# Hybrid decoder trunk on one core: the first norm's gain spread by GpSimd into SBUF instead of by one-row products into PSUM

## The chip, the core and the metric

The kernel runs on one core of a Trainium2 chip. The metric is the device time of one execution in microseconds (us), as the median of several runs; the inputs lie in the chip's memory at the start and the output has to be there at the end.

## What is computed

Two layers work on 256 rows of 1024 float32 values. Each layer is a half-weighted gated feed-forward block, a mixing block (retention, block attention and convolution heads side by side), and a second feed-forward block; a norm stands ahead of each block and one at the end. Cut to what the change touches:

```python
def rms_norm(x, g):
    y = x * lax.rsqrt(jnp.mean(x * x, -1, keepdims=True) + EPS)
    return y * g

for l in range(DEPTH):                                   # DEPTH = 2
    h = rms_norm(x, ffn1_norm[l])
    x = x + 0.5 * (jax.nn.silu(h @ ffn1_wg[l]) * (h @ ffn1_wu[l])) @ ffn1_wd[l]
    h = rms_norm(x, mix_norm[l])
    x = x + mix(h @ w_in[l], ...) @ w_out[l]
    h = rms_norm(x, ffn2_norm[l])
    x = x + 0.5 * (jax.nn.silu(h @ ffn2_wg[l]) * (h @ ffn2_wu[l])) @ ffn2_wd[l]
return rms_norm(x, final_norm)
```

The change lies in the very first `rms_norm`: its `g` is a vector of 1024 values that multiplies every row, so each of the 128 partitions needs a copy of it.

## The kernel before

The 256 rows are two tiles `x0` and `x1` of 128 partitions by 1024. Weights are float32 and come as "raw" buffers (three of them, up to 1 MB each) on SyncE's queue; ScalarE makes a rounded high part of each (`whi`), VectorE the remainder (`wlo`), and TensorE multiplies with both. All engines follow a written order in the opening; TensorE does so throughout.

The opening is `setup` and `start`. `setup` sets a small constant on GpSimd (`mhalf`), starts the loads of `x0` and `x1` in halves on SyncE's queue, and loads the gain (`row`, one partition of 1024) and the identity (`ident`) on ScalarE's queue. `start` then

- issues dummy products on TensorE (`spin`, a bf16 tile of ones `z` times itself), between them two one-row products, `ones` times `row`, that put the gain on 128 partitions in two PSUM banks `g[0]`, `g[1]` (line 260), and one more dummy;
- takes the sums of squares of each half tile on ScalarE (`stats`, line 271), and from them the row factor `r` on GpSimd in three small instructions, `e`, `e` and `r` (lines 272 to 274);
- multiplies x by `r` and `g` on VectorE (`rows`, line 280, output `xr`, one half tile each; there is one buffer `xr`, so the second tile's first half must wait until the transposes have read the first tile);
- transposes `xr` on TensorE (`turn`, line 286), and makes the high and low parts of the transposed rows, `hT` (lines 294 and 298);
- starts the first weight products (`prod`, line 326), with the eight pieces of the first two raw buffers split by lines 314 and 318.

After the opening the feed-forward block goes on with `single` and `down`, fed by `pump` (lines 147 and 148).

Of the kernel before, what the change touches and what calls it, by code (L numbers as in the profile page):

```python
# [11 lines left out]
F32 = mybir.dt.float32  # L12
# [8 lines left out]
D = 1024  # L21
S = 256
P = 128
# [32 lines left out]
class Kernel:  # L56
# [144 lines left out]
    def mm3(self, out, ah, al, wh, wl, start, stop):  # L201
        mm = self.nc.tensor.matmul
        mm(out, ah, wh, start=start, stop=False)  # L203
        mm(out, ah, wl, start=False, stop=False)  # L204
        mm(out, al, wh, start=False, stop=stop)  # L205

    def mm2w(self, out, wh, wl, x, start, stop):
        mm = self.nc.tensor.matmul
        mm(out, wh, x, start=start, stop=False)  # L209
        mm(out[:, :S], wl, x[:, 0], start=False, stop=stop)  # L210
# [12 lines left out]
    def setup(self):  # L223
        nc, c, a = self.nc, self.const, self.a
        self.mhalf = c.tile([P, 8], F32, tag="mhalf", name="mhalf")
        nc.gpsimd.memset(self.mhalf, -0.5)
        warm = c.tile([P, 8], F32, tag="warm", name="warm")
        nc.scalar.activation(warm, self.mhalf, AF.Silu)
        self.x = [c.tile([P, D], F32, tag=f"x{t}", name=f"x{t}") for t in range(NT)]
        for t in range(NT):  # L230
            for h in range(2):
                n = slice(h * 512, (h + 1) * 512)
                nc.sync.dma_start(self.x[t][:, n], a["x"][t][:, n])
        self.row = self.act.tile([P, D + 8], F32, tag="g", bufs=1, name="row")[0:1, :D]
        nc.scalar.dma_start(self.row, a["fgain"][0:1])
        self.ident = self.load("ident", (P, P), eng=nc.scalar)

# [1 line left out]
    def start(self, st):  # L241
        nc, mm = self.nc, self.nc.tensor.matmul
# [2 lines left out]
        n[0]["xr"] = n[0]["tile"]()  # L245
        sqs = [self.act.tile([P, 512], BF16, tag="sq", bufs=1, name=self.name("sq"))]
        z = self.scratch(BF16)
        ones = self.scratch()
        nc.vector.memset(z, 1.0)
        nc.vector.memset(ones[0:1, :P], 1.0)  # L250
        idle = self.mmb()

        def spin(n):
            for _ in range(n):
                mm(idle, z[:, :P], z, start=True, stop=True)

        spin(4)
        g = [self.acc() for _ in range(2)]
        for h in range(2):
            mm(g[h], ones[0:1, :P], self.row[:, h * 512:(h + 1) * 512], start=True, stop=True)  # L260
        spin(1)
        while len(self.raws) < RBUFS:
            self.fetch()

# [871 lines left out]
```

## Time and profile before

| | |
|---|---|
| median of 3 runs | 991.15 us (990.84 to 991.24) |
| profiled execution, its own time | 988.81 us |
| its span, first to last instruction | 987.0 us |
| TensorE busy | 976.8 us, 99% of the span |
| VectorE busy | 683.8 us, 69% |
| ScalarE busy | 537.1 us, 54% |
| GpSimd busy | 67.5 us, 7% |

The profiled execution took 1.8 us more than its span. A busy share near 100% on TensorE means that nearly every microsecond holds some product; it doesn't say that the product was needed, since the dummies of the opening count as well.

### The profile page before, as it was taken

How to read it: one execution, taken by the hardware profiler on the slowest of the kernel's cores; microseconds unless marked ns; L12 is line 12 of the kernel's file. 1: busy time of each engine (PE TensorE's matmuls, PEld its weight loads, DVE VectorE, ACT ScalarE, POOL GpSimd, SP SyncE). 2: the span in 40 equal slices, each digit the busy share in tenths (PEclk: the TensorE clock that was granted, in tenths of full speed). 3: DMA queues.
4: the chain of work that ended last, by engine and by line, in shares of the span. 5: the costliest groups of instructions: out<-in, count | busy, mean ns of one | idle time of the engine just before them, and what ended most of it. 6: DMA issues, size and time to landing. Idle time of an engine off the chain costs nothing.

```text
span 987.0 us, 13779 instructions
## 1 busy us (share of the span) xinstructions
PE 976.8 (99%) x5321; PEld 850.1 (86%) x5321; DVE 683.8 (69%) x1030; ACT 537.1 (54%) x904; POOL 67.5 (7%) x115
## 2 busy tenths in 40 slices
PE   9999999999999999999999999999999999999997
PEld 6888888898998888888888888888989888888885
DVE  5987565669976866666676656566799677666653
ACT  5755555366554755555465555554665456555542
POOL 0101000021140000000000000002100400000000
PEclk9999999999999999999999999999999999999999
DMA  7975555345542855555546464543545346555511
GB/s 258 334 273 178 205 180 180 119 152 190 171 171 70 309 199 174 208 175 206 176 183 223 171 210 173 205 142 136 193 144 199 135 151 254 176 208 173 209 45 43
DMA packets 28580, 180.17 MB, mean 183 GB/s; under 512 B 3425, under 2 KB 3809, under 8 KB 10338
## 3 DMA queue, kind: packets, MB, share of 16 engines
q1 hardware_dynamic: 27216, 175.54, 51.1%
q10 hardware_dynamic: 1298, 3.74, 1.0%
q8 instruction: 42, 0.69, 0.3%
q14 instruction: 24, 0.20, 0.1%
HBM read 178.22 MB, written 1.05 MB: 182 GB/s over the span
## 4 chain that ended last, share of the span: by engine, by line
PE 92%; DVE 5%; ACT 1%; DMA 1%; issue 1%; POOL 0%; SPq 0%; POOLq 0%; ACTq 0%; DVEq 0%
PE mm L209 15%; PE tr L209 15%; PE acc L614 8%; PE acc L613 8%; PE acc L617 8%; PE tr L210 8%; PE mm L210 8%; PE mm L203 4%; PE mm L205 4%; PE mm L204 4%; DVE wlo L148 2%; DVE ac L866 2%; PE acc L209 1%; PE mm L326 1%; PE tr L505 1%; PE acc L809 1%
## 5 line engine op out<-in xcount | busy, mean ns | idle before, releaser
L148 DVE TENSOR_TENSOR wlo<-raw,whi 128x1024 fp32r<-128x1024 f32 (+1 forms) x340 | 397.9, 1181 | 172.8 <-ACT whi L147 168.9
L147 ACT ACTIVATE whi<-raw 128x1024 fp32r<-128x1024 f32 (+1 forms) x340 | 344.0, 1023 | 213.1 <-PE acc L617 84.7
L209 PE MATMUL mm<-hT,whi 128*128 128x512 f32 x640 | 226.1, 391 | 0.0
L209 PE MATMUL tr<-hT,whi 128*128 128x512 f32 x640 | 225.9, 391 | 0.0
L210 PE MATMUL tr<-hT,wlo 128*128 128x256 f32 x640 | 180.5, 282 | 0.0
L210 PE MATMUL mm<-hT,wlo 128*128 128x256 f32 x640 | 180.4, 282 | 0.0
L209 PEld LDWEIGHTS mm<-hT,whi 128*128 128x128 f32 x640 | 120.1, 188 | 25.9
L209 PEld LDWEIGHTS tr<-hT,whi 128*128 128x128 f32 x640 | 120.1, 188 | 25.1
L613 PE MATMUL acc<-whi,hf 128*128 128x512 f32 x352 | 137.7, 391 | 0.0
L614 PE MATMUL acc<-wlo,hf 128*128 128x512 f32 x352 | 137.2, 390 | 0.0
L210 PEld LDWEIGHTS mm<-hT,wlo 128*128 128x128 f32 x640 | 120.8, 189 | 1.4
L210 PEld LDWEIGHTS tr<-hT,wlo 128*128 128x128 f32 x640 | 121.0, 189 | 0.0
L617 PE MATMUL acc<-whi,hf 128*128 128x512 f32 x352 | 113.6, 389 | 0.0
L203 PE MATMUL mm<-whi,hT 128*128 128x384 f32 (+1 forms) x272 | 99.3, 365 | 0.0
L205 PE MATMUL mm<-whi,hT 128*128 128x384 f32 (+1 forms) x272 | 94.2, 346 | 0.0
L204 PE MATMUL mm<-wlo,hT 128*128 128x384 f32 (+1 forms) x272 | 94.1, 346 | 0.0
L617 PEld LDWEIGHTS acc<-whi,hf 128*128 128x128 f32 x352 | 66.1, 188 | 13.9
L599 ACT ACTIVATE s<-part 128x256 f32<-128x256 f32 x80 | 33.2, 416 | 82.2 <-DVE part L215 82.0
L613 PEld LDWEIGHTS acc<-whi,hf 128*128 128x128 f32 x352 | 66.1, 188 | 13.6
L614 PEld LDWEIGHTS acc<-wlo,hf 128*128 128x128 f32 x352 | 66.2, 188 | 12.3
L215 DVE TENSOR_TENSOR part<-part,tr 128x256 f32<-128x256 f32 x80 | 33.5, 419 | 47.3 <-ACT part L214 47.3
L866 DVE SCALAR_TENSOR_TENSOR ac<-u,vec,ac 128x256 f32<-128x256 f32 x120 | 56.6, 525 | 0.0
(179 smaller groups left out, 983.2 us busy)
## 6 DMA issues: line engine op xcount, KB each, us to landing
raw<-in_wgb SPq DMA_DIRECT2D x80, 1024.0 KB, 4.9
raw<-in_wd SPq DMA_DIRECT2D x44, 1024.0 KB, 4.9
raw<-in_win SPq DMA_DIRECT2D x28, 768.0 KB, 5.1
raw<-in_wout SPq DMA_DIRECT2D x8, 1024.0 KB, 4.9
raw<-in_wga SPq DMA_DIRECT2D x6, 1024.0 KB, 5.4
raw<-in_wcv SPq DMA_DIRECT2D x4, 1024.0 KB, 5.0
raw<-in_wga SPq DMA_DIRECT2D x8, 256.0 KB, 5.6
g<-in_fgain ACTq DMA_DIRECT2D x3, 512.0 KB, 3.9
```

The source lines that it names most:

```text
L147: nc.scalar.activation(hi[:, c], src, AF.Copy)
L148: nc.vector.tensor_tensor(lo[:, c], src, hi[:, c].bitcast(F32), op=OP.subtract)
L203: mm(out, ah, wh, start=start, stop=False)
L204: mm(out, ah, wl, start=False, stop=False)
L205: mm(out, al, wh, start=False, stop=stop)
L209: mm(out, wh, x, start=start, stop=False)
L210: mm(out[:, :S], wl, x[:, 0], start=False, stop=stop)
L215: self.nc.vector.tensor_tensor(v, lo, ps[:, :S], op=OP.add)
L613: mm(ys[t][h], hi[:, ts], wh[:, n], start=first, stop=False)
L614: mm(ys[t][h], hi[:, ts], wl[:, n], start=False, stop=False)
L617: mm(ys[t][h], lo[:, ts], wh[:, n], start=False, stop=last)
L866: nc.vector.scalar_tensor_tensor(ac[ct], us, wj, ac[ct], op0=OP.mult, op1=OP.add)
```

## The change

The gain is now loaded as two rows of 512 into two scratch buffers, each by its own transfer on ScalarE's queue, and GpSimd's `partition_broadcast` copies each row to 128 partitions of an SBUF tile `g0`. The two one-row products, their PSUM banks and the tile `ones` are gone. `ident` is loaded behind the two rows. TensorE has 14 dummies in one piece, where it had four, the one-row products and one.

```diff
-        self.row = self.act.tile([P, D + 8], F32, tag="g", bufs=1, name="row")[0:1, :D]
-        nc.scalar.dma_start(self.row, a["fgain"][0:1])
-        self.ident = self.load("ident", (P, P), eng=nc.scalar)
+        self.g0 = self.act.tile([P, D + 8], F32, tag="g", bufs=1, name="g0")[:, :D]
...
         z = self.scratch(BF16)
-        ones = self.scratch()
         nc.vector.memset(z, 1.0)
-        nc.vector.memset(ones[0:1, :P], 1.0)
+        g = []
+        for h in range(2):
+            row = self.scratch()[0:1]
+            nc.scalar.dma_start(row, self.a["fgain"][0:1, h * 512:(h + 1) * 512])
+            g.append(self.g0[:, h * 512:(h + 1) * 512])
+            nc.gpsimd.partition_broadcast(g[h], row)
+        self.ident = self.load("ident", (P, P), eng=nc.scalar)
         idle = self.mmb()
...
-        spin(4)
-        g = [self.acc() for _ in range(2)]
-        for h in range(2):
-            mm(g[h], ones[0:1, :P], self.row[:, h * 512:(h + 1) * 512], start=True, stop=True)
-        spin(1)
+        spin(14)
```

GpSimd's row before, from `mhalf` to the row factors of both tiles. An `ISA` row without a tile here is the instruction that selects the library of GpSimd code; it is not written in the kernel but put in by the compiler.

```order
L226 MEMSET mhalf 128x8
L272 ISA
L272 TENSOR_SCALAR e_127<-ss_126 128x1 [waits Activation_49]
L273 TENSOR_TENSOR e_127<-ss_126,e_127 128x1 [waits Activation_49,Pool_49]
L274 TENSOR_TENSOR r_128<-e_127,mhalf 128x1 [waits Pool_49]
L272 TENSOR_SCALAR e_136<-ss_135 128x1 [waits Activation_49]
```

The same place after the change; the two `ISA` rows with `g` are the broadcasts, each of which waits for its row's transfer.

```order
L226 MEMSET mhalf 128x8
L252 ISA
L252 ISA g_84<-hf_90 128x512 [waits DMAHW3_49]
L252 ISA g_84<-hf_93 128x512 [waits DMAHW5_49]
L271 ISA
L271 TENSOR_SCALAR e_135<-ss_134 128x1 [waits Activation_49]
L272 TENSOR_TENSOR e_135<-ss_134,e_135 128x1 [waits Activation_49,Pool_49]
L273 TENSOR_TENSOR r_136<-e_135,mhalf 128x1 [waits Pool_49]
L271 TENSOR_SCALAR e_144<-ss_143 128x1 [waits Activation_49]
```

Ahead of the first `e` there now stand two broadcasts and a second selection: library 1 for the broadcasts, library 0 again for what follows, as before.

SyncE's queue before, the first loads of x and of the weights (`raw`); what a row waits for is the landing of an earlier transfer that used the same counter.

```order
L233 DMA x_78<-in_x 128x512 x2
L233 DMA x_79<-in_x 128x512 x2
L129 DMA raw_105<-in_wga 128x512 x2
L129 DMA raw_105<-in_wga 128x512 [waits DMAHW0_49]
L129 DMA raw_105<-in_wga 128x512 [waits DMAHW1_49]
L129 DMA raw_110<-in_wga 128x512 [waits DMAHW2_49]
```

The same place after the change.

```order
L233 DMA x_78<-in_x 128x512 x2
L233 DMA x_79<-in_x 128x512 x2
L129 DMA raw_113<-in_wga 128x512
L129 DMA raw_113<-in_wga 128x512 [waits DMAHW0_49]
L129 DMA raw_113<-in_wga 128x512 [waits DMAHW1_49]
L129 DMA raw_113<-in_wga 128x512 [waits DMAHW2_49]
```

ScalarE issues three transfers where it issued two, so the counters come round one place earlier: the second to fourth weight piece now each wait for the half of x one place later (counters 0 to 3 belong to the halves of x and to the gain's row). Behind the opening the engines' orders are the same in both kernels.

## Rows read from the trace of the kernel before

**Rows 1.** The page: span, busy time by engine, the chain that ended last.
```profile
span 987.0 us, 13779 instructions
PE 976.8 (99%) x5321; PEld 850.1 (86%) x5321; DVE 683.8 (69%) x1030; ACT 537.1 (54%) x904; POOL 67.5 (7%) x115
PE 92%; DVE 5%; ACT 1%; DMA 1%; issue 1%; POOL 0%; SPq 0%; POOLq 0%; ACTq 0%; DVEq 0%
```

**Rows 2.** Stretches: length, busy time and count by engine, clock, DMA.
```profile
24.00:200.00 176.00, 176.00 (x938) 152.72 (x938) 123.84 (x200) 98.94 (x164) 8.52 (x21) 1.00 0.59 206
```

**Rows 3.** Chain in the opening: start, length, what.
```profile
1.64 4.35 DMA x<-in_x
6.00 3.91 DMA raw<-in_wga
```

**Rows 4.** Timeline of VectorE: start, length, operation, idle time before it.
```profile
5.78 0.23 DVE L397 CAST ident<-ident 128x128 bf16<-128x128 f32 x1 [4.19 <-DMA ident<-in_ident]
6.58 0.75 DVE L280 SCALAR_TENSOR_TENSOR xr<-x,r,acc 128x512 f32<-128x512 f32 x1 [0.57 <-POOL r L274]
7.62 0.75 DVE L280 SCALAR_TENSOR_TENSOR xr<-x,r,acc 128x512 f32<-128x512 f32 x1 [0.30 <-PE acc L260]
9.92 0.75 DVE L280 SCALAR_TENSOR_TENSOR xr<-x,r,acc 128x512 f32<-128x512 f32 x1 [1.55 <-DMA raw<-in_wga]
```

**Rows 5.** Timeline of GpSimd in the opening.
```profile
0.72 0.10 POOL L226 MEMSET mhalf<- 128x8 f32 x1 [0.29 <-POOLq L1128]
4.89 0.23 POOL L272 TENSOR_SCALAR e<-ss 128x1 f32<-128x1 f32 x1 [4.07 <-ACT sq L271]
5.71 0.19 POOL L273 TENSOR_TENSOR e<-ss,e 128x1 f32<-128x1 f32 x1 [0.59 <-ACT sq L271]
5.97 0.57 POOL L274 TENSOR_TENSOR r<-e,mhalf 128x1 f32<-128x1 f32 x1
```

**Rows 6.** Line 272 by operation: ns min/median/max, first and last start.
```profile
L272 POOLq MODIFY_POOL_CONFIG  x2: 11/11/11, 0.8 to 0.8; - x2
```

**Rows 7.** DMA issues from 0 to 12 us, then 20 to 80: median us to landing.
```profile
raw<-in_wga SPq DMA_DIRECT2D x8, 256.0 KB, 5.6
ident<-in_ident ACTq DMA_DIRECT2D x1, 64.0 KB, 4.3
...
decay<-in_decay SPq DMA_DIRECT2D x1, 768.0 KB, 7.0
```

**Rows 8.** Groups of GpSimd instructions, shapes apart: busy us, mean ns, idle.
```profile
L888 POOL TENSOR_TENSOR hf<-hf,rstd 128x512 f32<-128x512 f32 x2 | 2.1, 1045 | 0.2
L468 POOL COPY rs<-sn 128x64 f32<-128x64 f32 x1 | 0.3, 272 | 0.0
```

**Rows 9.** Timeline of TensorE in the opening.
```profile
1.44 1.89 PE L255 MATMUL mm<-hf 128*128 128x512 bf16 x4 [1.44 <-DVE hf L249]
3.84 3.75 PE L260 MATMUL acc<-row,hf 1*128 1x512 f32 x4 [0.52 <-DMA row<-in_fgain]
7.52 0.61 PE L255 MATMUL mm<-hf 128*128 128x512 bf16 x1
7.92 1.92 PE L286 MATMUL tr<-ident,xr 128*128 128x128 f32 x8
11.90 0.60 PE L286 MATMUL tr<-ident,xr 128*128 128x128 f32 x4
```

**Rows 10.** Transposes of line 286, up to 10 us and from 11 us: ns.
```profile
L286 PE MATMUL tr<-ident,xr x8: 421/421/421, 7.9 to 9.4; 128*128 128x128 f32 x8
L286 PE MATMUL tr<-ident,xr x8: 272/273/273, 11.9 to 13.6; 128*128 128x128 f32 x8
```

**Rows 11.** Timeline of ScalarE in the opening.
```profile
0.71 1.28 ACT L228 ACT_TABLE_LOAD   x1 [0.71 <-PEq L1128]
0.86 0.53 ACTq L235 DMA_DIRECT2D row<-in_fgain  x1
8.37 0.63 ACT L314 ACTIVATE whi<-raw 128x512 fp32r<-128x512 f32 x1 [0.82 <-DMA raw<-in_wga]
```

## The prediction

> **What bounds the kernel now.** I read the page first: TensorE is busy for 976.8 of 987.0 us, and 92% of the chain that ended last is TensorE's [rows 1]. So I asked whether a stretch behind the opening has room in which a late start could be made good. From 24 to 200 us TensorE is busy for 176.00 of 176.00 us, at the full granted clock [rows 2]: whatever the opening loses or gains reaches the end undiminished, and the whole question is when the first useful products start. The chain in the opening begins with the load of x; it names a weight transfer as the next piece, from 6.00 us for 3.91 [rows 3]. I don't believe that weight transfer: VectorE's third `xr` at 9.92 follows the eight transposes, which end at 9.84 [rows 4, 9], and it writes the one buffer that they read. The true chain is: sums of squares, row factor `r`, first `xr`, transposes, third `xr`, and so on. The first `xr` starts at 6.58 us when GpSimd's `r` (5.97 plus 0.57) is there [rows 4, 5]. GpSimd, busy for 7% of the span, is therefore on the path at this one place.
>
> **The change, part by part.**
>
> *What it removes.* The one-row products hold TensorE from 3.84 to about 7.5 us [rows 9]. The second `xr` waits 0.30 us for the second of them [rows 4], and the transposes can't start before 7.92, though the first `xr` ends at 7.33.
>
> *What it adds on GpSimd.* Its queue is now: select library 1, broadcast, broadcast, select library 0, then `e`, `e`, `r`. Queued behind every one of these are the row factors of both tiles, and for them wait all four `xr`, all transposes and all products. Before, one selection stood there, two instructions of 11 ns at 0.8 us [rows 6], with nothing due before `e` at 4.89: whatever it set off lay within the 4.07 us in which GpSimd waited for ScalarE anyway [rows 5].
>
> The price of a switch to another library is shown nowhere. From below it is nothing (the instructions take 11 ns). If code has to be brought from memory, the nearest rows are transfers: 64 KB landed after 4.3 us in the opening, the eight 256 KB weight pieces after 5.6 us (median) in the same first 12 us, 768 KB after 7.0 us later [rows 7]. The 4.07 us of before bound it only if that selection was a real switch; if library 0 was in place already, since nothing before it had asked for another, they say nothing. Now the first selection differs from what stood last, and so does the second, so I take both as real. I take 5.6 us for each, the row of the transfers that are in flight in just this stretch, and keep 4.3 and 7.0 for the range.
>
> The GPSIMD Engine Reference of the Trainium skill (section 2.1, Instruction dispatch) says that the first call into a freshly loaded library costs some 6 us more, with no instruction for it in the profile. With its 5.95 us for each switch my sum would come out 0.7 us higher, an estimate by that page. The row of before speaks against it as far as it goes: `e` started 4.1 us after its selection.
>
> A broadcast of 512 values isn't in the trace either. The nearest rows are a product of two 128x512 tiles on GpSimd, 1.05 us, and a copy of 64 columns, 0.27 us [rows 8]. I take 1.05 for its 512 columns; 0.27 is the lower end.
>
> *The sum.* `mhalf` ends at 0.82. Library 1: 0.82 + 5.6 = 6.42; the gain's row had landed by 3.84 [rows 9], its second half now comes 0.53 later, one more issue on ScalarE [rows 11], so neither is waited for. Broadcasts: 6.42 + 2 x 1.05 = 8.52. Library 0: 14.12. Row factor: 0.23 for the first `e`, 0.26 from the second to `r`, 0.57 for `r`, 0.04 to VectorE [rows 4, 5], in all 1.10, without the waits for ScalarE, which has long been done. First `xr` at 15.22 instead of 6.58: 8.64 us late.
>
> *What is caught up.* From the first `xr` to the third it was 3.34 us [rows 4]. Now the second follows at once (ends at 1.50, counted from the first's start), and the transposes start behind the first (0.80). They lie 0.213 us apart ((1.92 - 0.42) / 7) [rows 9, 10]: four end their turn at 1.65, four more at 2.50, the last is out 0.21 later, and with 0.08 to VectorE the third `xr` starts at 2.79. That is 0.55 less. From there VectorE and TensorE go on as before. Net 8.1 us.
>
> *The clock and the dummies.* The page's clock column shows 1.00 everywhere, yet a transpose takes 421 ns up to 9.4 us and 273 from 11.9 on, and four of them come 0.11 us apart instead of 0.213 [rows 9, 10]: TensorE is at the low level (1.2 GHz) until the real work has gone on for some 4 us, in spite of the dummies and the one-row products, and then at the high one (2.4 GHz). The 14 dummies, 0.43 us apart as the first four ((1.89 - 0.61) / 3 with the length of one) [rows 9], last until 7.6 us or end sooner if the clock rises in them. But the first transpose then comes at 16.0, after an idle stretch of over 8 us. I take it that the clock is low again and rises about as long after the first transpose as before: nothing gained, nothing lost. Bounds: if it stayed high, eight transposes save 0.10 us each, 0.83; if it stayed low for four more us of products, at half speed these give 2.0 less work.
>
> *At nothing.* `ident` lands some 0.5 us later, one issue on ScalarE; the cast of it, which stands ahead of the first `xr` on VectorE, went at 5.78 [rows 4] and now comes at 6.3, hidden behind 15.22. On SyncE's queue the weight pieces two to four wait for a half of x one place later; all of the first weights should be there long before 15 us. If the switches cost nothing this cover is gone, and then the two delays are some tenths of a us each, and the first weight part, which waits for its transfer until 8.37 [rows 11], sets the pace. VectorE loses a memset of one row that nobody waited for.
>
> The profiled execution took 988.81 us, 1.8 over its span; plus 8.1 that is 996.9. It lies 2.34 below the median of the runs, 991.15, by which the change will be measured: **999.3 us**.
>
> **The rivals.**
>
> *A, the forecast: both switches fetch code, 4.3 to 7.0 us each.* With 4.3 the first `xr` comes at 12.62, net 5.5 later: 996.6. With 7.0 at 18.02, net 10.9: 1002.0. Broadcasts of 0.27 take off 1.6, the clock adds up to 2.0.
>
> *B: the selection of before was a real switch, and fitted into its 4.07 us.* For it: `e` started on time. Against it: nothing shows that it did anything. At 4.0 each the first `xr` comes at 12.02, net 4.9: 996.0. At the 1.28 us that ScalarE's table load takes [rows 11], the nearest load of code, the broadcasts are set by the rows' landing (3.84 and 4.37) and end at 5.94; then 1.28 and 1.10 give 8.32, net 1.2: 992.4.
>
> *C: a switch is free; the other side.* The broadcasts end at 5.94, first `xr` at 7.04, 0.46 later than before. The dummies end at 7.6, the first `xr` at 7.79, the transposes follow with no break, at the high level if the dummies have raised the clock: the second four start at 1.55 after the first `xr`, four at 0.109 and 0.16 for the last's way out give 2.15, and 0.08 more the third `xr`: 1.1 us caught up. Net 0.65 faster, 990.5. This needs switches below about 0.7 us. To be 2 us faster the products up to 11 us would have to gain as well, which the weights' landing hardly allows.
>
> *D: worse than A.* A switch takes longer than any transfer of the trace, or the clock stays low longer on top of A: above 1003.5.
>
> **How the numbers follow.** A measurement of this kernel can tell about 0.2% from no change, 2.0 us: up to 993.1 counts as the same, under 989.2 as faster. Chances: A 0.60, B 0.22, C 0.13, D 0.05. The likeliest is A, 999.3. The range goes down to 993.0, which takes in nearly all of B (down to switches of 1.6 us), and up to 1003.5, A's upper end with most of the clock's bound; it leaves out C, D and B's lowest end. Slower by over 0.2%: A, D and 0.18 of B, 0.83. Faster: 0.03 of C. Within: 0.14. A's own range is 995.0 to 1003.5.
>
> **What will show it.** GpSimd: a gap of 4 to 7 us between the selection at 0.8 and the first broadcast, another between the second broadcast and the first `e`, with ScalarE's sums done by 8 us. VectorE: first `xr` at 12.6 to 18 us, released by `r`; the third 2.8 us later. TensorE: dummies until about 7, then idle until the first transpose, at 421 ns. Behind the opening every instruction late by the same 5 to 11 us, up to the end. The forecast is wrong if `e` follows the second broadcast within 1 us (C), if the gaps are there but under 4 us (B), or if a later stretch takes the delay back.

## The result, and the profile after

The changed kernel takes 1005.37 us (median of 4 runs, 1004.23 to 1005.73), the kernel before 991.0 in the same comparison: a ratio of 1.0147, 95% interval 1.0135 to 1.0159. It is 14.4 us slower. The forecast was 999.3 with a range up to 1003.5: the direction was right, and the size lies outside the range.

The profiled execution took 1005.1 us. The page of the changed kernel (span, busy time by engine), against [rows 1]:

```profile
span 1003.3 us, 13790 instructions
PE 978.4 (98%) x5326; PEld 851.7 (85%) x5326; DVE 684.4 (68%) x1029; ACT 537.6 (54%) x904; POOL 69.6 (7%) x117
```

No engine works much more. TensorE's busy time rose by 1.6 us while the span grew by 16.3: nearly all of the loss is waiting. GpSimd's timeline in the opening shows where it lies (start, length, operation, idle time before it and what ended it), against [rows 5]:

```profile
0.72 0.10 POOL L226 MEMSET mhalf<- 128x8 f32 x1 [0.29 <-POOLq L1127]
7.87 1.48 POOL L252 PARTITION_BROADCAST g<-hf  x2 [7.05 <-ACT sq L270]
19.40 0.25 POOL L271 TENSOR_SCALAR e<-ss 128x1 f32<-128x1 f32 x1 [10.05 <-issue]
19.74 0.19 POOL L272 TENSOR_TENSOR e<-ss,e 128x1 f32<-128x1 f32 x1
20.00 0.59 POOL L273 TENSOR_TENSOR r<-e,mhalf 128x1 f32<-128x1 f32 x1
```

There are two gaps, 7.05 and 10.05 us. The first is put down to ScalarE's sums, which the broadcast doesn't read, so this releaser is wrong. The second is put down to nothing at all ("issue"). Each has a library selection at its start; the second of them in the view of line 271 (ns, then first and last start):

```profile
L271 POOLq MODIFY_POOL_CONFIG  x2: 127/127/127, 9.3 to 9.3; - x2
```

VectorE's timeline, against [rows 4]: the identity's cast, the first two `xr`, the third.

```profile
6.80 0.23 DVE L396 CAST ident<-ident 128x128 bf16<-128x128 f32 x1 [5.34 <-DMA ident<-in_ident]
20.63 1.42 DVE L279 SCALAR_TENSOR_TENSOR xr<-x,r,g 128x512 f32<-128x512 f32 x2 [13.60 <-POOL r L273]
23.50 0.75 DVE L279 SCALAR_TENSOR_TENSOR xr<-x,r,g 128x512 f32<-128x512 f32 x1 [1.45 <-PE tr L285]
```

The first `xr` starts at 20.63 instead of 6.58, 14.05 us late, released by `r`; the third 13.58 late. TensorE's timeline, against [rows 9]:

```profile
1.44 5.15 PE L258 MATMUL mm<-hf 128*128 128x512 bf16 x14 [1.44 <-DVE hf L246]
21.44 1.97 PE L285 MATMUL tr<-ident,xr 128*128 128x128 f32 x8 [14.85 <-DVE xr L279]
25.93 1.05 PE L285 MATMUL tr<-ident,xr 128*128 128x128 f32 x4
28.48 1.02 PE L285 MATMUL tr<-ident,xr 128*128 128x128 f32 x4
```

The dummies end at 6.6 us, then TensorE is idle for 14.85. The later groups of four transposes take 1.05 and 1.02 us, where the group at 11.90 took 0.60 before. The view by stretches has the reason in its clock column, the first number behind GpSimd's (length; busy time and count of TensorE, weight loads, VectorE, ScalarE, GpSimd; clock; DMA share; GB/s):

```profile
8.00:20.00 12.00, 0.00 (x0) 0.00 (x0) 0.00 (x0) 0.64 (x3) 1.79 (x4) 0.54 0.58 201
20.00:24.00 4.00, 2.56 (x10) 2.10 (x10) 1.91 (x3) 1.41 (x3) 2.50 (x4) 0.50 0.00 0
24.00:28.00 4.00, 3.65 (x11) 2.61 (x11) 3.07 (x6) 2.22 (x5) 0.00 (x0) 0.50 0.00 0
28.00:32.00 4.00, 4.00 (x18) 3.28 (x17) 3.37 (x7) 3.11 (x6) 0.00 (x0) 0.83 0.00 0
```

The granted clock is 0.50, the low level of 1.2 GHz, from 20 to 28 us. The level can't always be read from this column: in the kernel of the lone switches below it says 1.00 where eight transposes take 1.97 us as here, and only the lengths show the low level. The last two columns show that no transfer ran from 20 to 32 us: all first weights had landed. The chain's piece in which the 40 first products end (start, length), with which the opening is over:

```profile
29.50 9.10 PE mm L325 x40
```

They end at 38.60 us; the same piece of the chain before ended at 13.87 + 9.19 = 23.06. So the opening is 15.54 us later: 14.05 to the first `xr`, 0.47 caught up to the third, and 1.96 lost behind it (15.10 us from the third `xr` to the end of the 40 products, where it was 13.14).

The profiled executions differ by 16.3 us, the medians by 14.4. The profiled execution of the kernel before, 988.81, lies at the low end of its runs: in a later comparison the 24 runs spread from 988.36 to 991.91, with a median of 990.43.

### The profile page after: what moved, and what is told of

Same layout as the page of the kernel before. It is cut to its first block, busy times and chain, and to the rows that moved or that the text cites. A ratio compares the mean times of both kernels' runs of the same rounds, so it can differ in the third digit from the quotient of the medians.

```text
span 1003.3 us, 13790 instructions
## 1 busy us (share of the span) xinstructions
PE 978.4 (98%) x5326; PEld 851.7 (85%) x5326; DVE 684.4 (68%) x1029; ACT 537.6 (54%) x904; POOL 69.6 (7%) x117
## 3 DMA queue, kind: packets, MB, share of 16 engines
HBM read 178.22 MB, written 1.05 MB: 179 GB/s over the span
## 4 chain that ended last, share of the span: by engine, by line
PE 89%; DVE 6%; issue 2%; ACT 1%; DMA 1%; POOL 0%; SPq 0%; POOLq 0%; ACTq 0%; DVEq 0%
PE tr L209 14%; PE mm L209 14%; PE acc L613 8%; PE acc L612 8%; PE acc L616 8%; PE tr L210 8%; PE mm L210 7%; PE mm L203 4%; PE mm L205 3%; PE mm L204 3%; DVE wlo L148 3%; DVE ac L865 2%; PE acc L209 1%; PE mm L325 1%; PE tr L504 1%
```

## The experiments

The theory: both library switches are real, the first costs 7 us and the second 10, and TensorE's clock, which fell in the idle time, costs some 2 us more. The rivals: the first gap is the wait for the gain's rows; the broadcasts themselves end long after their recorded end; the clock costs nothing because VectorE sets the pace.

### The switch back taken away

The three small instructions of the row factor become copies; the sum of the halves, the epsilon and the power are left out.

```diff
-            nc.gpsimd.tensor_scalar(e, ss[:, 0:1], EPS, None, op0=OP.add)
-            nc.gpsimd.tensor_tensor(e, ss[:, 1:2], e, op=OP.add)
-            nc.gpsimd.tensor_tensor(r, e, self.mhalf[:, :1], op=OP.pow)
+            nc.gpsimd.tensor_copy(e, ss[:, 0:1])
+            nc.gpsimd.tensor_copy(e, ss[:, 1:2])
+            nc.gpsimd.tensor_copy(r, e)
```

> The changed kernel, with the three small GpSimd instructions e, e and r (for both tiles) replaced by copies of the same 128x1 columns, which need no library of GpSimd code; the sum of the halves, the epsilon and the power -0.5 are left out, so the factor is a column of the sums. The second library selection ahead of the factor is thereby gone, and nothing else. Theory (the switch back to library 0 is the 10 us in which GpSimd stood idle after the broadcasts): the first copy follows the second broadcast within 0.3 us, the first xr starts at 10.0 to 10.7 us instead of 20.6, and the time falls by 9.5 to 12.5 us, to 993 to 996 us. Rival (the broadcasts themselves end only about 10 us after their recorded end, and what follows waits for that): the copies start at about 19 us all the same, and the time stays at 1004 to 1006 us.

994.32 us, ratio 1.0046 (1.0031 to 1.0061) to the kernel before (989.88 in these rounds). GpSimd's timeline:

```profile
8.00 1.48 POOL L252 PARTITION_BROADCAST g<-hf  x2 [7.18 <-ACT sq L270]
9.31 0.29 POOL L271 COPY e<-ss 128x1 f32<-128x1 f32 x1
```

The copy follows the broadcasts at once, with no library selection at its line, and the first `xr` came at 10.13. The broadcasts are done when their record says so; the 10 us were the switch back. The 4.4 us that are left over the kernel before go with the first switch and the clock: the first `xr` is 3.55 us later than before (10.13 against 6.58), and the first eight transposes take 1.97 us, as in the changed kernel.

### One switch instead of two

The factors come first, with library 0, then one switch, then the broadcasts.

```diff
-            nc.gpsimd.partition_broadcast(g[h], row)
...
         stats(0)
         stats(1)
+        for out, row in g:
+            nc.gpsimd.partition_broadcast(out, row)
```

> The changed kernel with the two broadcasts behind the row factors of both tiles on GpSimd: library 0 first, as in the kernel before, then one switch to library 1 at about 8.5 us, then the broadcasts, and xr waits for these. One switch is on the path instead of two, and it falls where the 10 us one fell, while the first weights are landing. If the price belongs to the library (7 us for library 1, 10 for library 0): broadcasts at 15.5 to 17.1 us, first xr at 16.4 to 17.2, time 1001 to 1002.5 us. If it belongs to the place (slow while the weights come in): broadcasts from 18.5, first xr at 19.5 to 20.2, time 1004 to 1005.5. If the second gap had nothing to do with switches: first xr at about 10, time 992 to 995.

1002.59 us, ratio 1.0131 (1.0116 to 1.0146). The last factor and the broadcasts on GpSimd:

```profile
8.54 0.57 POOL L272 TENSOR_TENSOR r<-e,mhalf 128x1 f32<-128x1 f32 x1
18.58 1.48 POOL L329 PARTITION_BROADCAST g<-hf  x2 [9.47 <-issue]
```

A switch to library 1 takes 9.47 us here, where it took 7.05 at the start: the price goes with the place, not with the library. The first `xr` came at 19.41, just ahead of what that theory gave (19.5 to 20.2). The time is 1.4 to 2.9 us under what I had for it. Most of that is the clock, which was back within four us of work (1.00 from 24 to 28 us): from the third `xr` (22.52) to the end of the 40 products (35.66) it took 13.14 us as before the change, not 15.10.

### The switches alone

This is the kernel before, with a broadcast of 8 columns of a constant ahead of the factors.

```diff
+        tiny = self.small.tile([P, 8], F32, tag="tiny", name="tiny")
+        nc.gpsimd.partition_broadcast(tiny, self.mhalf[0:1, :8])
         idle = self.mmb()
```

> The kernel before, one-row products and all, with one broadcast of 8 columns of a constant on GpSimd ahead of the row factors: nothing of it is waited for but the two library switches that it brings. Theory (switches are the whole price): the small broadcast starts at 7 to 8 us though it waits for no transfer, the first e at 17 to 19 us, time 13 to 16 us over the kernel before, 1003 to 1007 us. Rival (the first gap of 7 us was the wait for the gain's rows, or the price goes with the 512 columns): the broadcast starts by 2 us, e by 12 at the latest, time under 998 us.

1003.24 us, ratio 1.0134 (1.0118 to 1.0149). GpSimd, and TensorE's first transposes:

```profile
8.19 0.28 POOL L252 PARTITION_BROADCAST tiny<-mhalf  x1 [7.37 <-issue]
17.86 0.25 POOL L274 TENSOR_SCALAR e<-ss 128x1 f32<-128x1 f32 x1 [9.40 <-issue]
...
19.90 1.97 PE L288 MATMUL tr<-ident,xr 128*128 128x128 f32 x8 [12.01 <-DVE xr L282]
```

The broadcast waits for no transfer and starts at 8.19 all the same. Eight columns that nobody reads bring nearly the whole loss, 13.4 us over the kernel before (989.88): neither the size of the broadcasts nor the gain's rows can be the cause.

### TensorE kept busy

The changed kernel has 78 dummies instead of 14.

```diff
-        spin(14)
+        spin(78)
```

> The changed kernel with 78 dummies instead of 14, so that TensorE is busy at full width until about 20 us, where the first xr comes. Theory (some 2 us of the loss are the low clock, since TensorE stands idle from 6.6 to 21.4 us): transposes 0.11 us apart from the start, granted clock 1.00 from 20 to 32 us, third xr 2.2 us after the first instead of 2.9, and the time falls by 2 to 3.3 us, to 1002 to 1003.5 us. Rival (VectorE and ScalarE set the pace of the opening, not TensorE's clock): clock 1.00 as well, but the time stays within 1 us of 1005.4.

1002.07 us, ratio 1.0127 (1.0110 to 1.0144). That is 3.3 us under the changed kernel's 1005.37 from the earlier comparison; against the kernel before, each in its own rounds, it is 12.2 us slower instead of 14.4. GpSimd's first `e`, TensorE's first transposes, and the third `xr` on VectorE:

```profile
18.80 0.25 POOL L271 TENSOR_SCALAR e<-ss 128x1 f32<-128x1 f32 x1 [9.32 <-issue]
21.04 1.11 PE L285 MATMUL tr<-ident,xr 128*128 128x128 f32 x8
22.25 0.75 DVE L279 SCALAR_TENSOR_TENSOR xr<-x,r,g 128x512 f32<-128x512 f32 x1 [0.80 <-PE tr L285]
```

0.60 us of the 3.3 can't be credited to the clock: the first `xr` came at 20.03 here, 0.60 earlier, behind a switch back of 9.32 us instead of 10.05. From the first to the third `xr` it takes 2.22 us instead of 2.87, and from there to the end of the 40 products (35.40) 13.15 instead of 15.10, as long as before the change (13.14). At the high level the opening is thus 0.65 + 1.95 = 2.6 us shorter by the profiles: that the clock has a share is shown.

### Why the second switch is dearer

First I put a second pair of switches behind the factors of the lone-switch kernel, where no transfer ran from 16 to 29 us, with a small instruction of library 0 as a mark.

```diff
         stats(1)
+        tiny = self.small.tile([P, 8], F32, tag="tiny", name="tiny2")
+        nc.gpsimd.partition_broadcast(tiny, self.mhalf[0:1, :8])
+        mark = self.small.tile([P, 8], F32, tag="mark", name="mark")
+        nc.gpsimd.tensor_scalar(mark, self.mhalf, 1.0, None, op0=OP.add)
```

> The kernel of the lone switches again (the kernel before with a broadcast of 8 columns ahead of the row factors), and behind the factors of both tiles a second broadcast of 8 columns and a small instruction of library 0 as a mark. That gives four switches: at 1 us, at 8.4 (while weights land), at 20.3 and behind it (from 20 to 28 us no transfer ran in the lone-switch run). Theory that the traffic of the weights makes the second switch dear (9.4 us against 7.2): the second broadcast comes 6.5 to 7.5 us after 20.3, at 27 to 28 us. Rival (the first switch of a program is cheap and all later ones cost 9.4 to 10 us): it comes at 29.5 to 30.5 us. The time should stay within 2 us of that run's 1003.2 us either way, since GpSimd has nothing due between its factors at 20 us and the copies at about 43.

One run, 1003.76 us. The four switches on GpSimd:

```profile
8.40 0.28 POOL L252 PARTITION_BROADCAST tiny<-mhalf  x1 [7.57 <-ACT sq L273]
19.18 0.25 POOL L274 TENSOR_SCALAR e<-ss 128x1 f32<-128x1 f32 x1 [10.50 <-issue]
27.80 0.28 POOL L333 PARTITION_BROADCAST tiny<-mhalf  x1 [6.18 <-issue]
35.20 0.26 POOL L335 TENSOR_SCALAR mark<-mhalf 128x8 f32<-128x8 f32 x1 [7.12 <-issue]
```

The third takes 6.18 us, the fourth 7.12: later ones are not dearer as such. The time lies within the lone-switch kernel's 1001.22 to 1003.79, so the second pair, for which nobody waits, shows no cost.

Only the third switch fell in quiet. The stretches of the second and the fourth have nearly the same traffic (columns as above, DMA share and GB/s at the end), and the prices are 10.50 and 7.12:

```profile
9.00:19.00 10.00, 0.00 (x0) 0.00 (x0) 0.00 (x0) 0.00 (x0) 0.00 (x0) 1.00 0.56 204
28.00:35.00 7.00, 7.00 (x35) 5.84 (x33) 6.06 (x10) 3.02 (x5) 0.08 (x1) 1.00 0.49 169
```

Then I held back the first weights of the changed kernel until the factors are there, by a small GpSimd copy of `r` into each raw buffer ahead of its load: same place, same direction, no traffic.

```diff
-        while len(self.raws) < RBUFS:
-            self.fetch()
...
         stats(1)
+        while len(self.raws) < RBUFS:
+            self.fetch(after=n[0]["r"])
```

> The changed kernel with the first three weight buffers loaded only after the row factors: their transfers wait for a small GpSimd copy behind r, so that no weight traffic runs while GpSimd switches from library 1 back to 0, at the same place and in the same direction as in the changed kernel. Theory (the weights' traffic makes that switch 10 us long): e follows the second broadcast after 6 to 7.2 us instead of 10, r is there at 16 to 18 us instead of 20.6. Rival (the second switch of a program, or the direction from 1 to 0, is dear by itself): 9.3 to 10.5 us as before. The time is not the measure here: the weights come in only after 17 us and the first products wait for them, so it stays at 1002 to 1009 us.

One run, 1005.72 us. The stretch from 8 to 16 us, and GpSimd's broadcasts and first `e`:

```profile
8.00:16.00 8.00, 0.00 (x0) 0.00 (x0) 0.00 (x0) 0.07 (x1) 1.48 (x2) 0.55 0.00 0
...
8.56 1.48 POOL L254 PARTITION_BROADCAST g<-hf  x2 [7.74 <-ACT sq L269]
17.58 0.25 POOL L270 TENSOR_SCALAR e<-ss 128x1 f32<-128x1 f32 x1 [7.55 <-issue]
```

Without the weights' loads (DMA share 0.00) the switch back takes 7.55 us instead of 10.05. That is a little over the 7.2 that I had allowed, and `r` is there at 18.8 instead of by 18, but it is far from the rival's 9.3. The same switch took 9.32, 9.40 and 10.50 us in the other kernels that load the weights at this place, so its price varies by over 1 us between profiles, and holding the loads back takes off 1.8 to 3.0 us.

How the loads lengthen the switch stays open. The mean traffic doesn't order the prices: the fourth switch above took 7.12 us at a share of about 0.49, the second 10.50 at 0.56 (there the transfers ended at 15 us, here they began at 31). And the first switch of this run took 7.74 us although the share from 0.82 to 7.9 us was only 0.48, where it was 0.78 in the changed kernel, whose first switch took 7.05.

### The rest of the change without GpSimd

VectorE, idle until the identity comes, spreads the rows by a shuffle; the 14 dummies stay.

```diff
-            row = self.scratch()[0:1]
-            nc.scalar.dma_start(row, self.a["fgain"][0:1, h * 512:(h + 1) * 512])
+            row = self.scratch()
+            nc.gpsimd.memset(row, 0.0)
+            src = self.a["fgain"][0]
+            nc.scalar.dma_start(row[::32], bass.AP(tensor=src.tensor, offset=src.offset + h * 512, ap=[[0, 4], [1, 512]]))
...
-            nc.gpsimd.partition_broadcast(g[h], row)
+            nc.vector.stream_shuffle(g[h], row, [0] * 32)
```

> The changed kernel without any library switch: the gain's two rows go to four partitions each, and VectorE, idle there, spreads each over all 128 with a shuffle inside its groups of 32 partitions; the 14 dummies stay. It tells what the rest of the change (gain in SBUF, no one-row products, dummies in one piece) is worth when GpSimd is left out. Theory (the switches, and the clock lost while waiting for them, are the whole loss): first xr at 6.5 to 7.0 us, third 2.2 to 2.9 us behind it instead of 3.34, and the time 0.5 to 2 us under that of the kernel before in the same rounds. Rival (something else in the change costs as well: the third transfer on ScalarE's queue, the later weight pieces, the later identity): 1 to 3 us over the kernel before, with the first weight part or the identity as what is waited for.

989.96 us, ratio 1.0000 (0.9991 to 1.0010) to the kernel before (990.43). Neither the theory's gain nor the rival's loss came. GpSimd's `r` and VectorE's timeline tell why:

```profile
5.71 0.57 POOL L275 TENSOR_TENSOR r<-e,mhalf 128x1 f32<-128x1 f32 x1
...
5.96 0.73 DVE L254 STREAM_SHUFFLE g<-hf 128x512 f32<-128x512 f32 x1
7.27 0.23 DVE L398 CAST ident<-ident 128x128 bf16<-128x128 f32 x1 [0.58 <-DMA ident<-in_ident]
7.42 1.41 DVE L281 SCALAR_TENSOR_TENSOR xr<-x,r,g 128x512 f32<-128x512 f32 x2
```

`r` was there at 6.28 and the second shuffle was done at 6.69, but the identity, now issued behind two gain transfers that wait for a memset (at 3.02 us, where it was 1.69 in the changed kernel), lands only at 7.2, and its cast stands ahead of the first `xr`. From there the third came 2.21 us later.

With 18 dummies (`spin(18)`):

> As the kernel with VectorE's shuffles, with 18 dummies instead of 14, to close the gap between the last dummy (about 6.5 us) and the first transpose (about 7.5). Theory that the gap lets the clock fall again: high clock at the first transposes here, and 0.5 to 1.5 us faster than with 14. Rival (the gap is too short to matter, or the dummies now delay the transposes): within 0.5 us of it or slower.

989.40 us, ratio 0.9991 (0.9982 to 1.0000): 0.56 us under the 14, which this many runs barely tell apart. The 11 runs spread over 1.7 us instead of 3.1. In the profiles the first eight transposes take 1.32 us with 18 dummies as with 14, and TensorE is idle ahead of them for 1.58 us instead of 0.78, so the gap was not closed there, and nothing shows that the clock brought the 0.56.

With the gain spread by the transfer itself:

```diff
-            nc.scalar.dma_start(row, self.a["fgain"][0:1, h * 512:(h + 1) * 512])
-            nc.gpsimd.partition_broadcast(g[h], row)
+            src = self.a["fgain"][0]
+            nc.scalar.dma_start(g[h], bass.AP(tensor=src.tensor, offset=src.offset + h * 512, ap=[[0, P], [1, 512]]))
```

> The changed kernel with the gain spread by the transfer itself, as the later norms of this kernel do it: two transfers of 256 KB on ScalarE's queue whose source repeats for all 128 partitions, no GpSimd library, 14 dummies. 512 KB more go through ahead of x and the weights, at the 313 GB/s that the kernel before moved there some 1.7 us more. Theory: first xr at 7.5 to 8.5 us, time 0 to 1.7 us over the kernel before. Rival (the added bytes overlap with the wait for x and cost nothing): same as the kernel with VectorE's shuffles to 0.5 us.

993.23 us, ratio 1.0025 (1.0015 to 1.0035), 2.8 us more and beyond my 1.7. With the added bytes x lands later: ScalarE's third sum of squares waits for it until 9.19 us, where it started at 6.07 before. The identity lands later still, and VectorE's first `xr` starts behind its cast at 9.46, though `r` was there at 8.28.

```profile
9.19 0.63 ACT L269 ACTIVATE sq<-x 128x512 bf16<-128x512 f32 x1 [1.89 <-DMA x<-in_x]
9.31 0.23 DVE L395 CAST ident<-ident 128x128 bf16<-128x128 f32 x1 [7.86 <-DMA ident<-in_ident]
```

By then TensorE has been idle for 3.14 us, and the first eight transposes take 1.97 us, the low level again.

### A version that beats both

The identity first on ScalarE's queue, the gain into the target tile and shuffled in place, 16 dummies.

```diff
+        self.ident = self.load("ident", (P, P), eng=nc.scalar)
         g = []
         for h in range(2):
-            row = self.scratch()[0:1]
-            nc.scalar.dma_start(row, self.a["fgain"][0:1, h * 512:(h + 1) * 512])
             g.append(self.g0[:, h * 512:(h + 1) * 512])
-            nc.gpsimd.partition_broadcast(g[h], row)
-        self.ident = self.load("ident", (P, P), eng=nc.scalar)
+            nc.gpsimd.memset(g[h], 0.0)
+            src = self.a["fgain"][0]
+            nc.scalar.dma_start(g[h][::32], bass.AP(tensor=src.tensor, offset=src.offset + h * 512, ap=[[0, 4], [1, 512]]))
+            nc.vector.stream_shuffle(g[h], g[h], [0] * 32)
...
-        spin(14)
+        spin(16)
```

> The kernel with VectorE's shuffles, tidied: the identity is loaded ahead of the gain on ScalarE's queue, the gain lands in four partitions of the target tile itself (cleared by GpSimd first) and is shuffled in place, and there are 16 dummies. In the run with the shuffles the identity landed at 7.2 us and held the first xr until 7.42, 1.1 us behind r. Theory (that wait is what ate the gain of the shuffles): first xr at 6.3 to 6.8 us, third at 8.5 to 9.2, and the time 1 to 2.5 us under the kernel before in the same rounds. Rival (the landing of the weight pieces, or VectorE's row of eight weight parts, sets the pace anyway): first xr as early, but the time within 0.7 us of the 18-dummy run's 989.4.

988.33 us, ratio 0.9984 (0.9975 to 0.9993) to the kernel before (990.67). VectorE:

```profile
4.01 0.23 DVE L397 CAST ident<-ident 128x128 bf16<-128x128 f32 x1 [2.55 <-DMA ident<-in_ident]
6.07 0.73 DVE L254 STREAM_SHUFFLE g<-g 128x512 f32<-128x512 f32 x1
6.69 1.40 DVE L280 SCALAR_TENSOR_TENSOR xr<-x,r,g 128x512 f32<-128x512 f32 x2
8.89 0.75 DVE L280 SCALAR_TENSOR_TENSOR xr<-x,r,g 128x512 f32<-128x512 f32 x1 [0.80 <-DMA raw<-in_wga]
```

The third `xr` starts at 8.89 us instead of 9.92 [rows 4]. The kernel is 2.3 us faster by the medians and 0.16%, 1.6 us, by the ratio, with an interval clear of 1. So the gain that the change was after is there, once GpSimd doesn't spread the rows. The three edits were made together; which of them brings how much isn't shown.

## Why the prediction was wrong

*The bound.* Right: a late first product is paid in full. From the end of the 40 products to the end of the span it took 964.7 us (1003.3 - 38.60) and before 963.9 (987.0 - 23.06); no later stage took anything back.

*The mechanism.* Right: two real switches, the first not hidden, the second on the path with everything behind it. The selection of before was no real switch, or a cheap one, since every switch measured here took 6.18 us or more: the 4.07 us that rival B rested on bounded nothing. (The range's lower end, 993.0, answers to switches of 1.9 us, not of 1.6.)

*The step that failed* is the price of the switches: "I take 5.6 us for each". It was 7.05 and 10.05. With the broadcasts at 1.48 together instead of 2.10 and the factor at 1.23 instead of 1.10 the sum is 0.82 + 7.05 + 1.48 + 10.05 + 1.23 = 20.63, the first `xr` as measured, 5.41 over my 15.22; the second switch alone makes 4.45 of it. The nearest row, transfers in the same stretch, was the wrong measure: even with no traffic a switch takes 6.2 to 7.6 us, more than the 4.3 and 5.6 us of the opening's transfers [rows 7], and while the first weights load the one behind it took 9.3 to 10.5. My upper end of 7.0 for a switch was the price of one in quiet, so the range ended too early. That the price differs by place was no term of my sum at all, and why it does is only shown in part: held-back weights took off 2.5 us in one pair of profiles. What came is rival D, to which I had given 0.05: a switch longer than the dearest transfer of [rows 7] (10.05 us against 7.0), and a clock that stays low longer. The page that I weighed, the GPSIMD Engine Reference of the Trainium skill (section 2.1), with its 5.95 us, is close to the switch in quiet from library 0 to 1 (6.18 us); no run here bears it out for a switch while the first weights load, where 9.3 to 10.5 were measured.

*What is caught up.* Right: the third `xr` came 2.87 us after the first, forecast 2.79.

*The clock.* "Nothing gained, nothing lost" was wrong by a smaller amount. It did fall in the idle time, as I had it, but it was still low at 28 us, over 6 us after the first transpose, where I had taken about 4: 1.96 us lost behind the third `xr`. The bound that I gave, 2.0, held. In the kernel with the factors first it rose within 4 us (0.54 from 20 to 24, 1.00 after), so the delay of the rise is not the same each time. The opening's 15.54 us are the forecast's 8.09 plus 5.41 from the switches' sum, 0.08 from the catching up and 1.96 from the clock.

*At nothing.* The identity came at 6.8, not at 6.3, and was hidden, as said. In the kernel with VectorE's shuffles, where it was issued 1.3 us later still, it held the first `xr` from about 6.7, when the second shuffle was done, to 7.42. That is not the price that rival C put at "some tenths"; no run here has the cheap switches of C.

*The base.* I added the delay to the median of the runs; the delay itself was worked out on the profiled execution, which lies 2.3 us below that median. By the profiles it is 16.3, by the medians 14.4. The 0.8 us between the opening's 15.5 and the span's 16.3 lie behind the opening and stay unexplained; at 305 us the delay is still 15.6 (GpSimd's `e` there starts at 320.67 instead of 305.11).

## What to carry to other kernels

Look at the order of GpSimd's queue for instructions that select a library: one operation from another library brings two switches, there and, as soon as an operation of the old library follows, back. Each took 6.2 to 10.5 us here, in which everything queued on GpSimd stands still, and the one back is easily on the path. A pair came to 13 to 18 us; only where GpSimd has nothing due for that long can it be hidden. For spreading one row over the partitions, an idle VectorE did it in 0.73 us per 512 columns without that price. And dummies that keep TensorE's clock up helped only where they went on nearly to the first real work: 14 that ended 14.85 us ahead of it did not, 78 that went on to it did.

## What the runs showed of the hardware

- The switch of GpSimd's library leaves instructions of 11 to 127 ns in the profile and 6.18 to 10.50 us of idle time put down to "issue" or to a wrong releaser. With a DMA share of 0.00 it took 6.18 (to library 1) and 7.55 us (back). At the start, while x landed, it took 7.05 to 7.74; behind that, while the first weights landed, 9.32 to 10.50; and one back from 28 to 35 us, with transfers from 31 us on, took 7.12.
- Copies of one column ran under library 1 with no switch (the kernel without the switch back); `tensor_scalar`, the first instruction of the factor, stood behind one.
- A broadcast of 512 columns to 128 partitions took 0.74 us (two in 1.48).
- GpSimd's small instructions for the second tile took 0.78 and 0.55 us in the changed kernel instead of 0.22 and 0.19 before. They ran beside VectorE's `xr`, which now reads both inputs from SBUF. With the gain in PSUM (the lone switches) they took 0.22 and 0.19 beside the same `xr`. In the changed kernel they ended 0.08 and 0.05 us behind the first and the second `xr`; in the kernel with the gain spread by the transfer, an `e` that started 0.53 us into such an `xr` took 0.29 us and ended 0.07 behind it. So the reason may be a wait for the `xr`, which no run here tests. It was not on the path here.
